# A tile for the attention sinks of 192 instead of 64 bytes: every tile behind it lies 128 bytes further on

## The chip, the cores and the metric

The kernel runs on one core of one Trainium2 chip. A core has a matrix engine (TensorE, "PE" in the profile, with its weight loads listed apart as "PEld"), a vector engine (VectorE, "DVE"), a scalar engine (ScalarE, "ACT"), GpSimd ("POOL") and SyncE ("SP", which only issues transfers here). They share an on-chip memory of 128 partitions, in which the program places its tiles by byte address within the partition, the same in all 128. The metric is the device time in microseconds of one execution; lower is better.

## The reference

The program computes two layers of a decoder trunk on 512 tokens of width 1024, in float32. Layer 0 mixes by sliding-window attention (8 query heads, 2 key heads, a learned sink per query head in the softmax's denominator) beside a short gated convolution; layer 1 by gated linear attention. Each layer then adds a gated MLP and a gated per-layer embedding:

```python
def _conv_ffn(h, w_up, conv_w, conv_b, w_down):
    u = _causal_depthwise_conv(h @ w_up, conv_w) + conv_b      # 1024 -> 2 * 2816
    gate, up = jnp.split(u, 2, axis=-1)
    return (jax.nn.gelu(gate, approximate=False) * up) @ w_down  # 2816 -> 1024
```

The sinks are eight numbers. In the softmax they are one more score per head, which has no value row.

## The kernel before

**Products in three.** A float32 operand is held as two tiles of the type float32r: a rounded high part and the rest. A product is three matmuls in a row (high by high, high by low, low by high): `mm3`, lines 162 to 168, which are lines 166, 167 and 168 of the profile. In each, the *stationary* operand (128 by 128, usually weights) is loaded into TensorE and the *moving* operand (128 partitions by 512 or 256 columns, usually activations of 512 or 256 tokens) streams past it. In the profile's groups the moving operand's tile stands first behind the arrow and the stationary one second: `ps<-four,wh` is a matmul whose moving operand lies in a tile named `four`.

**The MLP's up-projection** (`ffn`, from line 906) goes over 11 groups of 256 + 256 output columns per layer. The value half of a group is done plainly: two 128-column outputs, 8 blocks of the inner dimension each, three matmuls of 512 columns (`value`, line 950). The gate half goes through a Strassen-Winograd scheme with seven products in place of eight (`seven`, line 860): each product takes four blocks of three matmuls of 256 columns, 12 matmuls, at lines 875 to 877. Three of the seven products stream the plain normalised activations, which lie in the tiles `a0`, `a1` in layer 0 and `b0`, `b1` in layer 1; the other four stream sums and differences of them, the forms `s1` to `s4`, which `operand` (line 784) writes into tiles named `four`. TensorE's order is the order of the code (`manual_schedule` on PE); the other engines' order is a planner's.

**The down-projection** (`down`, line 1091) takes 22 activations. Those of number 0 to 7 are split into the tiles `uh` and `ul`, those of 8 to 21 into tiles `four` (`split_pair`, line 998). Numbers 0 to 13 are multiplied plainly, 512 columns a matmul. Numbers 14 to 21 go through `seven` again for four of the four column blocks in layer 0 and three of four in layer 1; there three of the seven products stream `four` tiles and four stream forms that lie in `a0`, `a1` (layer 0) or `b0`, `b1` (layer 1).

**The embedding's gate** (`ple0`, line 1284, and `ple1`, line 1326). In `ple0` the projected embedding streams from the tiles `ph0`, `pl0`, `ph1`, `pl1` of that stage's own pool. In `ple1` the weights are the moving side: half of their pieces lie in `wh`, `wl` and half in `four` tiles (`chunk`, line 1344), and `four` holds the stationary side of the projections (`proj`, line 1391).

**Where the tiles lie.** Tiles come from pools, and pools lie one behind the other in each partition. The pools `cp`, `xp`, `fp` (the `a0`, `a1`, `b0`, `b1`, `uh`, `ul` tiles), `wp` (`raw`, `wh`, `wl`), `sp` and `sm` live through the whole program; `sm` is the last of them and holds the small tiles of 32 bytes (`few`, line 79) and the sinks' tile (line 497). Behind `sm` lies the pool of whichever stage runs: `m0`, `ffn0`, `ple0`, `m1`, `ffn1`. The tiles in front of `sm` are all placed at multiples of 256 bytes, but for `mhalf`, the first, whose 128 bytes follow on 128 bytes of the program's own constants. The weights of the seven products are shifted within their tiles on purpose: `BLOCKS = (16, 48)` (line 58) puts the high part 64 bytes and the low part 192 bytes behind such a multiple (`cut_blocks`, line 812); all other weights start on one.

In `sm` there are 4 + 2 + 2 small tiles in front of the sinks', the sinks' 64 bytes, and 5 times 2 small tiles behind it: 256 + 64 + 320 = 640 bytes, which is 2.5 times 256. The pool of the running stage therefore begins at byte 157,312 = 614.5 times 256. All tiles of these pools are whole multiples of 256 bytes, so that every one of them starts 128 bytes behind a multiple of 256.

```python
def four(self, pool, dtype=F32R):                                        # line 97
    return pool.tile([P, 4, S], dtype, tag="four", name=self.nm("four"), bufs=7)

sink = self.sm.tile([P, 16], F32, name="sink", bufs=1)[:, :NQ]            # line 497
```

Of the kernel before, what the change touches and what calls it, by code (L numbers as in the profile page):

```python
# [9 lines left out]
F32 = mybir.dt.float32  # L10
# [8 lines left out]
P = 128  # L19
# [7 lines left out]
NQ, NKV, HD = 8, 2, 64  # L27
# [33 lines left out]
class Kernel:  # L61
# [367 lines left out]
    def mixer0(self):  # L429
        nc, a, tc = self.nc, self.a, self.tc  # L430
        with tc.tile_pool(name="m0", bufs=1) as mp:
# [62 lines left out]
            self.end_norm(sums=sums)  # L494
            with tc.issue_after(last[1].ins):
                C, Sn = self.rope_tables(mp)
            sink = self.sm.tile([P, 16], F32, name="sink", bufs=1)[:, :NQ]
            self.late(sink[:, :1])
            nc.gpsimd.dma_start(sink, a["hy_sinks"][0:1, :].partition_broadcast(P))
            nc.vector.tensor_scalar_mul(sink, sink, -1.0)  # L500
# [1476 lines left out]
```

## Time and profile before

| | |
|---|---|
| median of 3 runs | 1211.8 us (1211.75 to 1212.57) |
| profiled execution, its own time | 1211.79 us |
| its span, first to last instruction | 1210.0 us |
| TensorE busy | 1203.6 us (99%), 7018 matmuls |
| VectorE busy | 969.4 us (80%) |
| ScalarE busy | 667.9 us (55%) |
| GpSimd busy | 44.7 us (4%) |
| granted TensorE clock | 1.000 |

The span lacks 1.8 us of the execution's own time, which lie before the first and behind the last instruction. A matmul's duration in the profile reaches from its start to the modelled end of its pipeline, so that matmuls in a row overlap: 0.28 us stands for one of 256 columns while the next one starts 0.12 us later. How fast TensorE goes is read from the starts in the timeline, not from the durations.

### The profile page before, as it was taken

What the parts mean: (1) busy time and instruction counts of PE and PEld (TensorE: products, weight loads), DVE (VectorE), ACT (ScalarE), POOL (GpSimd) and SP (SyncE); (2) the same over time, 40 slices, a digit from 0 to 9 for tenths busy, and PEclk for the clock granted to TensorE, in tenths of its full rate; (3) what the DMA queues carried; (4) which work ended last, traced back from release to release, by engine and by line L of the source; (5) the groups of instructions that cost most, each with busy time, mean ns of one, the idle gap of its engine ahead of it and who ended that gap; (6) DMA issues with size and microseconds to landing.
All of it is one profiled execution on the core that took longest, in us unless ns stands there. A gap on an engine that the chain in (4) does not pass through costs nothing.

```text
span 1210.0 us, 17728 instructions
## 1 busy us (share of the span) xinstructions
PE 1203.6 (99%) x7018; PEld 1042.1 (86%) x7018; DVE 969.4 (80%) x1543; ACT 667.9 (55%) x1093; POOL 44.7 (4%) x64
## 2 busy tenths in 40 slices
PE   9999999999999999999999999999999999999998
PEld 8877789999999889888988988889999999888887
DVE  6786687899989986746679876778999898978595
ACT  7466565656554643534563654555665555645374
POOL 2600000000000000000100000000000000000000
PEclk9999999999999999999999999999999999999999
DMA  7232222324242332232322212322232423322501
GB/s 221 76 101 70 73 70 77 133 71 139 71 139 70 127 114 86 92 105 80 111 93 69 77 64 71 104 87 88 88 123 70 140 70 131 122 87 100 206 1 70
DMA packets 111128, 117.61 MB, mean 97 GB/s; under 512 B 2841, under 2 KB 106323, under 8 KB 111045
## 3 DMA queue, kind: packets, MB, share of 16 engines
q1 hardware_dynamic: 109680, 115.35, 28.8%
q8 instruction: 55, 0.90, 0.3%
q0 software_dynamic: 560, 0.42, 0.2%
q10 hardware_dynamic: 804, 0.70, 0.2%
q14 instruction: 29, 0.23, 0.1%
HBM read 114.37 MB, written 2.10 MB: 96 GB/s over the span
## 4 chain that ended last, share of the span: by engine, by line
PE 95%; DVE 3%; ACT 1%; issue 0%; ACTq 0%
PE ps L166 14%; PE ps L167 14%; PE ps L168 14%; PE pa L167 7%; PE pa L166 7%; PE pa L168 7%; PE ps L875 6%; PE ps L876 6%; PE ps L877 6%; PE pa L875 2%; PE pa L876 2%; PE pa L877 2%; PE ps L1374 1%; PE ps L1373 1%; PE ps L1372 1%; DVE wl L147 1%
## 5 line engine op out<-in xcount | busy, mean ns | idle before, releaser
L146 ACT ACTIVATE wh<-raw 128x1024 fp32r<-128x1024 f32 (+4 forms) x154 | 152.4, 992 | 150.4 <-PE ps L167 103.2
L147 DVE TENSOR_TENSOR wl<-raw,wh 128x1024 fp32r<-128x1024 f32 (+4 forms) x154 | 175.1, 1138 | 56.4 <-ACT wh L146 55.6
L822 ACT ACTIVATE wh<-raw 128x1024 fp32r<-128x1024 f32 x78 | 82.7, 1061 | 124.0 <-DVE raw L847 65.8
L935 DVE SCALAR_TENSOR_TENSOR zt<-z,vfa,zt 128x510 f32<-128x510 f32 (+1 forms) x176 | 130.6, 744 | 11.7 <-ACT zt L933 11.2
L823 DVE TENSOR_TENSOR wl<-raw,wh 128x1024 fp32r<-128x1024 f32 x78 | 95.3, 1222 | 20.6 <-ACT wh L822 20.5
L933 ACT ACTIVATE zt<-z,vfb 128x512 f32<-128x512 f32 x88 | 71.0, 809 | 23.9 <-DVE four L986 12.8
L166 PE MATMUL ps<-b,wh 128*128 128x512 f32 x192 | 76.6, 399 | 0.0
L167 PE MATMUL ps<-b,wh 128*128 128x512 f32 x192 | 75.1, 391 | 0.0
L168 PE MATMUL ps<-b,wl 128*128 128x512 f32 x192 | 74.9, 390 | 0.0
L167 PE MATMUL pa<-a,wh 128*128 128x512 f32 x176 | 69.1, 392 | 0.0
L167 PE MATMUL pa<-b,wh 128*128 128x512 f32 x176 | 69.0, 392 | 0.0
L166 PE MATMUL pa<-a,wh 128*128 128x512 f32 x176 | 68.8, 391 | 0.0
L166 PE MATMUL pa<-b,wh 128*128 128x512 f32 x176 | 68.8, 391 | 0.0
L168 PE MATMUL pa<-a,wl 128*128 128x512 f32 x176 | 68.7, 390 | 0.0
L168 PE MATMUL pa<-b,wl 128*128 128x512 f32 x176 | 68.6, 390 | 0.0
L876 PE MATMUL ps<-four,wh 128*128 128x256 f32 x232 | 65.3, 281 | 0.0
L875 PE MATMUL ps<-four,wh 128*128 128x256 f32 x232 | 65.1, 281 | 0.0
L877 PE MATMUL ps<-four,wl 128*128 128x256 f32 x232 | 64.8, 279 | 0.0
L166 PE MATMUL ps<-a,wh 128*128 128x512 f32 x160 | 63.6, 398 | 0.0
L167 PE MATMUL ps<-a,wh 128*128 128x512 f32 x160 | 62.4, 390 | 0.0
L168 PE MATMUL ps<-a,wl 128*128 128x512 f32 x160 | 62.4, 390 | 0.0
L166 PE MATMUL ps<-uh,wh 128*128 128x512 f32 x128 | 50.2, 392 | 0.0
(472 smaller groups left out, 3500.6 us busy)
## 6 DMA issues: line engine op xcount, KB each, us to landing
raw<-in_ffn_w_up_dram SPq DMA_DIRECT2D x44, 1024.0 KB, 5.0
raw<-in_ffn_w_down_dram SPq DMA_DIRECT2D x13, 1024.0 KB, 4.7
raw<-in_hy_w_in_dram SPq DMA_DIRECT2D x8, 1024.0 KB, 4.9
raw<-in_gla_w_in_dram SPq DMA_DIRECT2D x8, 1024.0 KB, 5.0
raw<-in_ffn_w_down_dram SPq DMA_DIRECT2D x8, 768.0 KB, 4.1
raw<-in_ple_w_gate_dram SPq DMA_DIRECT2D x6, 1024.0 KB, 4.6
raw<-in_hy_w_out_dram SPq DMA_DIRECT2D x16, 256.0 KB, 4.0
raw<-in_gla_w_out_dram SPq DMA_DIRECT2D x4, 1024.0 KB, 4.6
```

The source lines that it names most:

```text
L146: nc.scalar.activation(hv, v, AF.Copy)
L147: nc.vector.tensor_tensor(lv, v, hv.bitcast(F32), ALU.subtract)
L166: mm(out, lh, rh, start=start, stop=False, **kw)
L167: mm(out, lh, rl, start=False, stop=False, **kw)
L168: mm(out, ll, rh, start=False, stop=stop, **kw)
L822: nc.scalar.activation(h, src, AF.Copy)
L823: nc.vector.tensor_tensor(l, src, h.bitcast(F32), ALU.subtract)
L875: mm(out, wh, xh, start=first and j == 0, stop=False, **kw)
L876: mm(out, wh, xl, start=False, stop=False, **kw)
L877: mm(out, wl, xh, start=False, stop=j == ND // 2 - 1, **kw)
L933: nc.scalar.activation(y, z, AF.Identity, scale=w2[:, f : f + 1], bias=bb[:, f : f + 1])
L935: nc.vector.scalar_tensor_tensor(out=y[:, tap:], in0=z[:, : S - tap], scalar=w[:, f : f + 1], in1=y[:, tap:], op0=ALU.mult, op1=ALU.add,)
```

## The change

The sinks' tile asks for 48 numbers per partition in place of 16, of which 8 are used as before. It grows from 64 to 192 bytes.

```diff
@@ -494,7 +494,7 @@
             self.end_norm(sums=sums)
             with tc.issue_after(last[1].ins):
                 C, Sn = self.rope_tables(mp)
-            sink = self.sm.tile([P, 16], F32, name="sink", bufs=1)[:, :NQ]
+            sink = self.sm.tile([P, 48], F32, name="sink", bufs=1)[:, :NQ]
             self.late(sink[:, :1])
             nc.gpsimd.dma_start(sink, a["hy_sinks"][0:1, :].partition_broadcast(P))
             nc.vector.tensor_scalar_mul(sink, sink, -1.0)
```

No instruction is added, removed or resized. The ten small tiles behind the sinks' in `sm` and every tile of the pools `m0`, `ffn0`, `ple0`, `m1` and `ffn1` lie 128 bytes further on: the pool of the running stage begins at byte 157,440 = 615 times 256, and its tiles start at multiples of 256 bytes. The tiles in front of the sinks' stay where they are.

## The prediction

> **What bounds the kernel now.** I read the page first: busy times and the chain that ended last.
>
> ```profile
> PE 1203.6 (99%) x7018; PEld 1042.1 (86%) x7018; DVE 969.4 (80%) x1543; ACT 667.9 (55%) x1093; POOL 44.7 (4%) x64
> PE 95%; DVE 3%; ACT 1%; issue 0%; ACTq 0%
> ```
>
> TensorE is the path nearly throughout. Next the waits of TensorE alone (who waited for whom, total, times, longest), here the first two of four, and then three stretches (busy us of PE, PEld, DVE, ACT, POOL): one group of the up-projection of layer 0, and the first 20 us of its down-projection.
>
> ```profile
> PE pa L201 <- DVE mhalf L190: 1.3, 1, 1.3
> PE pa L167 <- DVE wl L1352: 0.4, 1, 0.4
> ```
>
> ```profile
> 290.45:311.26 20.81, 20.81 (x133) 18.83 (x132) 18.79 (x26) 10.71 (x16) 0.00 (x0) 1.00 0.30 102
> ...
> 415.00:425.00 10.00, 10.00 (x45) 8.13 (x45) 9.99 (x15) 4.92 (x7) 0.00 (x0) 1.00 0.46 158
> 425.00:435.00 10.00, 10.00 (x45) 8.04 (x44) 10.00 (x18) 5.84 (x8) 0.00 (x0) 1.00 0.30 105
> ```
>
> In the MLP TensorE is paced by its own matmuls. A group of the up-projection takes 20.81 us, of which VectorE works 18.79: two us of slack, no more. At the start of the down-projection VectorE is full, too.
>
> The third view is the timeline of TensorE, read by starts. Three kinds of stretches are compared: a product of 12 matmuls on `four`, the same on `a`, and 16 blocks (48 matmuls of 512 columns) on `uh` and `ul`, then on `four`.
>
> ```profile
> 301.60 0.28 PE L875 MATMUL ps<-four,wh 128*128 128x256 f32 x1
> ...
> 303.02 0.28 PE L875 MATMUL ps<-a,wh 128*128 128x256 f32 x1
> ...
> 304.39 0.40 PE L166 MATMUL pa<-a,wh 128*128 128x512 f32 x1
> ...
> 308.50 0.28 PE L875 MATMUL pa<-a,wh 128*128 128x256 f32 x1
> ...
> 309.88 0.40 PE L166 MATMUL pa<-a,wh 128*128 128x512 f32 x1
> ...
> 408.46 0.40 PE L166 MATMUL ps<-uh,wh 128*128 128x512 f32 x1
> ...
> 418.69 0.39 PE L166 MATMUL ps<-uh,wh 128*128 128x512 f32 x1
> ...
> 419.37 0.40 PE L166 MATMUL ps<-four,wh 128*128 128x512 f32 x1
> ...
> 430.56 0.40 PE L166 MATMUL ps<-four,wh 128*128 128x512 f32 x1
> ```
>
> The product on `four` takes 303.02 - 301.60 = 1.42 us, the next one on `a` 1.37, and another on `a`, behind matmuls of 512 columns as the first is, 1.38. The weights come from the same tiles at the same two offsets (64 and 192), and the shapes are equal. At 512 columns 48 matmuls take 10.91 us on `uh` and `ul` (227.3 ns each) and 11.19 on `four` (233.1 ns). So whatever streams from `four` goes about 4 ns a matmul slower at 256 columns and 6 at 512.
>
> What sets `four` apart? By the addresses its tiles start at 128 behind a multiple of 256, those of `a`, `b`, `uh`, `ul` on one. The groups by shape show whether other tiles follow that line (busy us, mean ns; a triple's other two lines have the same counts):
>
> ```profile
> L876 PE MATMUL ps<-four,wh 128*128 128x256 f32 x232 | 65.3, 281 | 0.0
> L876 PE MATMUL ps<-a,wh 128*128 128x256 f32 x120 | 33.3, 278 | 0.0
> L876 PE MATMUL pa<-four,wh 128*128 128x256 f32 x116 | 32.6, 281 | 0.0
> L167 PE MATMUL ps<-ul,wh 128*128 128x512 f32 x128 | 50.1, 391 | 0.0
> L167 PE MATMUL ps<-four,wh 128*128 128x512 f32 x112 | 44.2, 395 | 0.0
> L876 PE MATMUL ps<-four,t 128*128 128x256 f32 x88 | 24.8, 282 | 0.0
> ...
> L167 PE MATMUL ps<-wl,a 128*128 128x512 f32 x32 | 12.5, 390 | 0.0
> ...
> L168 PE MATMUL pa<-wh,four 128*128 128x512 f32 x16 | 6.3, 395 | 0.0
> ...
> L167 PE MATMUL ps<-pl,wh 128*128 128x512 f32 x16 | 6.3, 394 | 0.0
> ...
> L1373 PE MATMUL ps<-four,a 128*128 128x512 f32 x14 | 5.5, 394 | 0.0
> ...
> L1373 PE MATMUL ps<-four,b 128*128 128x512 f32 x12 | 4.7, 395 | 0.0
> ...
> L1373 PE MATMUL ps<-wl,a 128*128 128x512 f32 x12 | 4.7, 390 | 0.0
> ```
>
> Every group with an operand in a shifted pool shows 394 to 395 ns at 512 columns, also `pl`, of another pool and stage, and also `pa<-wh,four`, where `four` is the stationary side. Groups wholly in front of the small pool show 390 to 391. Two points bear on the cause. The tiles `wl` start at 0, 256 and 512 behind a multiple of 2048, and stream at 390: 256 is alignment enough, and `four` will have that. And the last two blocks before 419.37 stream a `ul` that lies in a tile `R` of the pool `sp`, at 152,576, only 4,736 bytes in front of the first `four`: 419.37 - 418.69 = 0.68 us a block, the quick pace. A border by height in the memory would have to fall by chance between those two.
>
> **The change part by part.** Nothing is issued anew, removed or queued differently, and no wait is added; only addresses move.
>
> *The 256-column products on `four`.* 232 + 116 + 88 = 436 per line, three lines: 1308 matmuls, 109 products of 12. Each goes from 1.42 us to 1.37 or 1.38: 0.04 to 0.05 saved, 4.4 to 5.5 us in all; I take 4.9. In the up-projection that is four products a group, 0.18 us, so a group falls to about 20.63 us, still 1.8 above VectorE's 18.79. It counts in full there.
>
> *The 512-column matmuls with a shifted moving tile in the down-projection and in `ple0`.* 3 x 112 + 3 x 16 = 384. By the rows' means 395 against 391 less what rounding hides, say 3 ns, by the timeline 5.8: 1.2 to 2.2 us; I take the middle, 1.7.
>
> *`ple1`.* 3 x (14 + 12) moving and 3 x 16 stationary, 126 matmuls, 4 to 6 ns each: 0.5 to 0.7 us where TensorE paces the stage. The wait of 0.4 us above lies there, so part may be lost: 0 to 0.7, taken 0.3.
>
> *VectorE and ScalarE on shifted tiles.* Nothing:
>
> ```profile
> L857 DVE TENSOR_TENSOR raw<-raw 128x512 f32<-128x512 f32 x26 | 17.8, 685 | 0.1
> ...
> L932 DVE TENSOR_TENSOR z<-z,R 128x512 f32<-128x512 f32 x22 | 15.0, 682 | 0.0
> ```
>
> `raw` is aligned, `z` shifted, and the two times agree within 3 ns. The slack of 2 us a group would cover it; without that cover 3 ns on some 20 operations is 0.06 us a group.
>
> *Plain float32 matmuls of the mixers* (attention's scores, the linear attention's levels, transposes). The nearest rows compare a transpose of an aligned tile with one of a shifted tile:
>
> ```profile
> L1380 PE MATMUL pa<-cf,xT 128*128 128x128 f32 x32 | 4.1, 272 | 0.0
> L1827 PE MATMUL pa<-cf,sc 128*128 128x128 f32 x32 | 4.1, 272 | 0.0
> ```
>
> No difference, so I take 0. The bound: these groups hold some 500 records; at 5.8 ns either way that is 2.9 us.
>
> *Transfers into shifted tiles.* At the start x lands in `xin`, which moves, among pieces of the weights for `raw`, which doesn't (same size, median us to landing):
>
> ```profile
> xin<-in_x_dram SPq DMA_DIRECT2D x8, 256.0 KB, 4.8
> ...
> raw<-in_hy_w_in_dram SPq DMA_DIRECT2D x4, 256.0 KB, 5.7
> ```
>
> The shifted ones land no later than the aligned ones. I take 0, and 0.9 us either way as the bound.
>
> The sum: 4.9 + 1.7 + 0.3 = 6.9 us. The profiled execution's own time is 1211.79 (its span 1210.0 and 1.8 around it), the median of the runs 1211.8, so the sum needs no correction: **1204.9 us**.
>
> One rule speaks against all this. The Trainium skill, "SBUF — State Buffer", section "Specifications (TRN2)", gives the memory lines of 16 bytes, and its section "Who interferes with whom" gives TensorE two independent read ports and says that it waits on nobody. By that a start at 128 is as good as one at 0, and the sum would be 0 and the time 1211.8. The rows above (1.42 against 1.37 us) don't fit it, since both kinds of product read whole lines of 16 bytes.
>
> **The rivals.**
>
> *The gain is made and given back* (VectorE takes over). For it: the two full rows of the down-projection, 9.99 and 10.00 of 10 us. There VectorE makes the forms that the products at 443 us need, and TensorE arriving 0.3 us sooner may wait for them; ScalarE's copies between products may eat as much again in each of the seven column blocks that run by `seven`. Against it: no wait of TensorE on VectorE in that stretch in the list. I price it as all of the 512-column gain and a fifth of the other: 4.9 x 0.8 + 0.3 = 4.2, so 1207.6 us.
>
> *Nothing happens.* The change wouldn't do what it says if `four` were slow for where it is and not for its phase: for its height in the memory. For it: all shifted tiles are also the highest ones, and no tile of the profile is high and aligned. Against it: the `ul` at 152,576. The time is 1211.8 us. The skill's lines of 16 bytes would end here, too.
>
> *Equal phases collide: slower.* Moving and stationary operands that both start on a multiple of 256 are read together in the keys' and values' projection, where `wh` streams past `a`. Twelve matmuls of 256 columns in a row, from the timeline:
>
> ```profile
> 17.10 0.28 PE L168 MATMUL pa<-wh,a 128*128 128x256 f32 x1
> ...
> 18.54 0.28 PE L168 MATMUL pa<-wh,a 128*128 128x256 f32 x1
> ```
>
> 1.44 us for 12, worse than the 1.42 on the shifted `four`. If the products on `four` came to that pace and the 512-column ones gained nothing, the price would be 109 x 0.02 = 2.2 us: 1214.0. It decides once a product takes longer than 1.42. Against it: the weights of the products stand at 64 and 192, so that phases never become equal there, and with 512 columns `uh` and `wh` have equal phases and run at 227.3 ns.
>
> **How the numbers follow.** The forecast gets 0.80, the gain given back 0.10, nothing 0.07, slower 0.03. A measurement of this kernel tells about 0.2% (2.4 us) from no change. The forecast and the first rival lie beyond that: faster 0.90. Nothing, and most of the collision at +2.2 us, lie within: I put 0.08 there and 0.02 on slower. The range goes down to 1202.8, where the two main terms come at their upper ends (5.5 and 2.2), `ple1` at 0.7, and 0.6 of the unseen bounds helps, and up to 1208.5, where the gain is given back and the start costs its bound of 0.9 more.
>
> **What would show it.** In the changed kernel's timeline a product on `four` should take 1.37 to 1.38 us and 48 matmuls of 512 columns on `four` about 10.9 us; a group of the up-projection about 20.63 us; the groups `ps<-four`, `ps<-pl` and `pa<-wh,four` should read 390 to 392 ns at 512 columns. VectorE's and ScalarE's means should stay as they are. If the products stay at 1.42 us, the phase isn't the cause, and the forecast falls. If they quicken and the time doesn't, TensorE must show new waits, first in the down-projections.

## The result and the profile after

The changed kernel takes **1205.3 us** (median of 6 runs, 1204.9 to 1205.7) beside 1211.8 us before (6 runs): a ratio of 0.9946, 95% interval 0.9935 to 0.9957. The profiled execution took 1205.4 us with a span of 1203.6, against 1211.79 and 1210.0 before. Every engine has the same instructions in the same order.

The page of the changed kernel, busy times and the chain that ended last; below it TensorE's waits (total, times, longest), in full:

```profile
PE 1196.3 (99%) x7018; PEld 1036.0 (86%) x7018; DVE 968.4 (80%) x1543; ACT 665.5 (55%) x1093; POOL 44.7 (4%) x64
...
PE 82%; DVE 12%; DMA 2%; ACT 2%; issue 1%; ACTq 0%; DVEq 0%
```

```profile
PE pa L201 <- DVE mhalf L190: 1.3, 1, 1.3
PE ps L875 <- ACT ps L896: 0.7, 3, 0.3
PE pa L167 <- DVE wl L1352: 0.6, 1, 0.6
PE ps L166 <- DVE kT L1564: 0.2, 1, 0.2
PE pa L167 <- DVE wl L147: 0.2, 1, 0.2
```

TensorE is 7.3 us less busy. TensorE's share of the chain falls from 95% to 82% and VectorE's rises from 3% to 12%. The second wait is new: a product waits for a copy that ScalarE makes from one accumulator to another (L896). In ScalarE's queue that copy stands behind the gelu (L1064), which had waited for VectorE, as here for the wait at 317 us:

```profile
316.01 1.06 ACT L1064 ACTIVATE zt<-zt 128x1024 f32<-128x1024 f32 x1 [1.08 <-DVE zt L935]
316.98 0.37 ACT L896 COPY ps<-ps 128x256 f32<-128x256 f32 x1
```

So something was given back.

The timeline of TensorE after, by starts: a product on `four` behind matmuls of 512 columns, block by block, the product on `a` behind it, and 16 blocks of 512 columns on `four` in the down-projection.

```profile
279.43 0.28 PE L875 MATMUL ps<-four,wh 128*128 128x256 f32 x1
279.79 0.28 PE L875 MATMUL ps<-four,wh 128*128 128x256 f32 x1
280.13 0.28 PE L875 MATMUL ps<-four,wh 128*128 128x256 f32 x1
...
280.81 0.28 PE L875 MATMUL ps<-a,wh 128*128 128x256 f32 x1
...
282.18 0.40 PE L166 MATMUL pa<-a,wh 128*128 128x512 f32 x1
...
417.70 0.39 PE L166 MATMUL ps<-four,wh 128*128 128x512 f32 x1
...
428.58 0.39 PE L166 MATMUL ps<-four,wh 128*128 128x512 f32 x1
```

The product on `four` takes 280.81 - 279.43 = 1.38 us (1.42 before), the one on `a` 1.37, as before. The 48 matmuls of 512 columns take 10.88 us (11.19 before), 226.7 ns each. The groups by shape agree:

```profile
L876 PE MATMUL ps<-four,wh 128*128 128x256 f32 x232 | 64.2, 277 | 0.0
...
L167 PE MATMUL ps<-four,wh 128*128 128x512 f32 x112 | 43.6, 390 | 0.0
...
L168 PE MATMUL pa<-wh,four 128*128 128x512 f32 x16 | 6.3, 391 | 0.0
...
L167 PE MATMUL ps<-pl,wh 128*128 128x512 f32 x16 | 6.2, 389 | 0.0
```

Now five groups of the up-projection of layer 0, the third to the seventh, cut at the starts of their first products (length and busy us of PE, PEld, DVE, ACT, POOL). First before (the third and the fifth), then after (all five):

```profile
228.01:248.82 20.81, 20.81 (x133) 18.83 (x132) 20.22 (x29) 12.33 (x19) 0.00 (x0) 1.00 0.31 102
...
269.64:290.45 20.81, 20.81 (x133) 18.83 (x132) 20.75 (x30) 13.69 (x21) 0.00 (x0) 1.00 0.31 102
```

```profile
227.29:247.87 20.58, 20.58 (x133) 18.63 (x132) 19.99 (x28) 12.35 (x18) 0.00 (x0) 1.00 0.31 103
247.87:268.46 20.59, 20.59 (x133) 18.62 (x132) 20.00 (x29) 11.83 (x17) 0.00 (x0) 1.00 0.31 103
268.46:289.05 20.59, 20.59 (x134) 18.63 (x132) 20.53 (x30) 13.26 (x20) 0.00 (x0) 1.00 0.32 103
289.05:309.87 20.82, 20.82 (x134) 18.54 (x132) 18.75 (x25) 10.51 (x14) 0.00 (x0) 1.00 0.31 102
309.87:331.23 21.36, 21.10 (x133) 18.62 (x132) 19.27 (x26) 11.27 (x17) 0.00 (x0) 1.00 0.30 100
```

Most groups now take 20.59 us, 0.22 less than before. But VectorE has no room in the fifth: 20.53 of 20.59 us. The two groups behind it take 20.82 and 21.36 us; the first of them shows no idle time of TensorE, because modelled durations overlap, so the list of waits (0.7 us) tells less than the lengths do. Layer 1 shows the same shape (20.72 and 21.17 us), and there the last group with the plain down-projection takes 48.48 us, where layer 0's takes 47.74.

Two questions follow. Is the quicker pace due to where the moving operand starts, as the prediction has it? And does VectorE open the new waits?

### The profile page after: what moved, and what is told of

Its sections match the earlier page's. It is cut to its first block, busy times and chain, and to the rows that moved or that the text cites. A ratio compares the mean times of both kernels' runs of the same rounds, so it can differ in the third digit from the quotient of the medians.

```text
span 1203.6 us, 17728 instructions
## 1 busy us (share of the span) xinstructions
PE 1196.3 (99%) x7018; PEld 1036.0 (86%) x7018; DVE 968.4 (80%) x1543; ACT 665.5 (55%) x1093; POOL 44.7 (4%) x64
## 4 chain that ended last, share of the span: by engine, by line
PE 82%; DVE 12%; DMA 2%; ACT 2%; issue 1%; ACTq 0%; DVEq 0%
PE ps L166 14%; PE ps L167 14%; PE ps L168 14%; PE pa L167 5%; PE pa L166 5%; PE pa L168 5%; PE ps L875 4%; PE ps L877 4%; PE ps L876 4%; DVE zt L935 3%; DMA raw<-in_ffn_w_up_dram 2%; DVE wl L823 2%; PE pa L875 2%; PE pa L877 2%; PE pa L876 2%; DVE wl L147 1%
## 5 line engine op out<-in xcount | busy, mean ns | idle before, releaser
L935 DVE SCALAR_TENSOR_TENSOR zt<-z,vfa,zt 128x510 f32<-128x510 f32 (+1 forms) x176 | 130.7, 744 | 11.7 <-ACT zt L933 11.2
```

What stands on the lines that cost most here:

```text
L935: nc.vector.scalar_tensor_tensor(out=y[:, tap:], in0=z[:, : S - tap], scalar=w[:, f : f + 1], in1=y[:, tap:], op0=ALU.mult, op1=ALU.add,)
```

## The experiments

Times are medians. The kernel before ran beside each and gave 1211.5 to 1211.8 us. "Phase" is a start in the memory modulo 256.

**Other phases of the moved tiles.** The kernel before, with a sinks' tile of 32, of 64 and of 80 numbers. The stage's pools then start at phase 192, at 64, and at 128 again but 256 bytes higher than before.

```diff
-            sink = self.sm.tile([P, 16], F32, name="sink", bufs=1)[:, :NQ]
+            sink = self.sm.tile([P, 32], F32, name="sink", bufs=1)[:, :NQ]   # 64; 80
```

> The sinks' tile has 128 bytes: the stage pools begin 192 behind a multiple of 256 (kernel before: 128, changed kernel: 0). Theory A (a moving operand that starts anywhere inside a stretch of 256 bytes needs one stretch more): as slow as before, 1211 to 1212.5 us, a product of 12 on `four` 1.42 us. Theory C (the cost shrinks with the distance to the next multiple, or the unit is 64 bytes): 1205 to 1209 us, a product at 1.37 to 1.40.

> The sinks' tile has 256 bytes: the stage pools begin 64 behind a multiple of 256. Theory A: 1211 to 1212.5 us, a product on `four` 1.42 us. Theory C: between 1205 and 1211 us. A result unlike that at 192 would mean that the phase against the weights' 64 and 192 matters, not the start alone.

> The sinks' tile has 320 bytes: everything behind it lies 256 bytes further on than in the kernel before, at the same phase of 128. Theory A: as before, 1211.8 us (1211.3 to 1212.3), a product on `four` 1.42 us. If the unit were 512 bytes or more, or if any shift away from the old place helped: under 1209 us.

Measured: 1211.97 us at 192 (ratio 1.0003, 0.9993 to 1.0012), 1213.19 at 64 (1.0012, 1.0003 to 1.0021), 1211.46 at 128 higher up (0.9998, 0.9988 to 1.0007). A product on `four`, the product on `a` behind it and the next matmul, first at 192, then at 64:

```profile
300.91 0.28 PE L875 MATMUL ps<-four,wh 128*128 128x256 f32 x1
...
302.32 0.28 PE L875 MATMUL ps<-a,wh 128*128 128x256 f32 x1
...
303.72 0.40 PE L166 MATMUL pa<-a,wh 128*128 128x512 f32 x1
```

```profile
302.25 0.28 PE L875 MATMUL ps<-four,wh 128*128 128x256 f32 x1
...
303.68 0.28 PE L875 MATMUL ps<-a,wh 128*128 128x256 f32 x1
...
305.10 0.39 PE L166 MATMUL pa<-a,wh 128*128 128x512 f32 x1
```

On `four` 1.41 and 1.43 us: neither phase brings the gain. The rival of height fell with the result, since the quick tiles lie higher than the slow ones did; the third run adds that a move by itself changes nothing. But the products on `a` are slower too, 1.40 and 1.42, and `a` was not moved. At 256 columns a matmul's own moving start can't be the whole cause.

At 512 columns the picture is another. The groups by shape, first at 192, then at 64:

```profile
L167 PE MATMUL ps<-four,wh 128*128 128x512 f32 x112 | 44.2, 394 | 0.0
...
L168 PE MATMUL pa<-wh,four 128*128 128x512 f32 x16 | 6.3, 393 | 0.0
```

```profile
L167 PE MATMUL ps<-four,wh 128*128 128x512 f32 x112 | 43.6, 390 | 0.0
...
L168 PE MATMUL pa<-wh,four 128*128 128x512 f32 x16 | 6.3, 395 | 0.0
```

By the starts of the first 72 matmuls on `four` in layer 0's down-projection, one takes 233.2 ns with `four` at 128, 233.3 at 192, 229.2 at 64 and 226.7 at 0. So a start at 64 brings more than half of the gain at 512 columns, and the loss on the products of 256 columns outweighs it. The weights of these matmuls start on multiples of 256 in every run here. In `pa<-wh,four` it is the other way round: the moving `wh` starts on such a multiple and `four` is the stationary side. That group reads 391 ns with `four` at 0, 395 at 64 and 128, and 393 at 192. As distances (the stationary start less the moving one, modulo 256) the two agree: 0 is quick, 192 lies between, 64 and 128 are slow. The differences are of a few ns, and no run was made to test this.

**Which tiles bring the gain.** An unused tile of 128 bytes at the head of the MLP's pools alone: in the kernel before it moves those pools (`ple1` works in the second one) and nothing else, in the changed kernel it moves them back.

```diff
-            self.mlp = fp
+            self.mlp = fp; fp.tile([P, 32], F32, name=f"pad{i}")
```

> Sinks' tile as before; an unused tile of 128 bytes stands first in the two MLP pools, so that only the tiles of `ffn0` and `ffn1` start on multiples of 256, while those of `m0`, `ple0` and `m1` stay at 128. Theory A: nearly the whole gain, less 0.3 us for `ple0` and what the start of the program moved: 1205.4 to 1206.2 us. If the mixers or the transfers of x carried part of the gain: above 1207 us.

> The mirror image: the changed kernel with an unused tile of 128 bytes first in the two MLP pools, so that `m0`, `ple0` and `m1` start on multiples of 256 and only the MLP's tiles at 128. Theory A: 1211.0 to 1211.8 us (gain 0.3 of `ple0` at most and a few tenths at the start). If mixers or transfers carried part: under 1210.5 us.

Measured: the MLP alone 1205.52 us (0.9949, 0.9935 to 0.9964), all but the MLP 1211.67 us (1.0001, 0.9991 to 1.0010). The gain is that of the MLP's pools. In the second kernel the groups by shape show the two pools apart:

```profile
L167 PE MATMUL ps<-four,wh 128*128 128x512 f32 x112 | 44.2, 395 | 0.0
...
L167 PE MATMUL ps<-pl,wh 128*128 128x512 f32 x16 | 6.2, 389 | 0.0
```

`ple0` has the quick pace and the MLP has not; `ple0`'s 48 matmuls at some 5 ns are 0.2 us, too little to show in the time.

**The weights' two places exchanged**, in the kernel before.

```diff
-BLOCKS = (16, 48)
+BLOCKS = (48, 16)
```

> The kernel before (`four` at 128) with the high and low parts of the product's weights exchanged in their offsets: high at 192, low at 64. Measured from the moving operand, each part then lies as in the changed kernel (64 and 192 further on). Theory A (the moving operand's own start): 1211.3 to 1212.3 us, products on `four` at 1.42. Theory R (the distance between the two operands): 1205 to 1207 us, products on `four` at 1.37 to 1.38.

Measured: 1208.79 us (0.9977, 0.9968 to 0.9986).

```profile
300.90 0.28 PE L875 MATMUL ps<-four,wh 128*128 128x256 f32 x1
...
302.28 0.28 PE L875 MATMUL ps<-a,wh 128*128 128x256 f32 x1
...
303.70 0.40 PE L166 MATMUL pa<-a,wh 128*128 128x512 f32 x1
```

With `four` still at 128, its product takes 1.38 us; `a`, at 0, takes 1.42. So an operand at 128 can go at the quick pace and one at 0 at the slow. For the products of 256 columns the cause that the prediction gave falls here. (The 72 matmuls of 512 columns keep their 233.2 ns; their weights don't use these places.) I put another in its place: what counts is the distance between the stationary and the moving start, modulo 256.

**Equal phases**, in the changed kernel: the weights' places at 0, as the moving operands are.

```diff
-BLOCKS = (16, 48)
+BLOCKS = (0, 0)
```

> The changed kernel with the offsets of the products' weights at 0 and 0 in place of 64 and 192, so that moving and stationary operands both start on multiples of 256. Theory E (equal phases collide with 256 columns, as in the keys' and values' projection at 1.44 us for 12): all 203 products go from 1.37 to 1.44 us, 1215 to 1220 us. If only the moving operand's start counts: 1205 to 1206 us.

Measured: 1215.73 us (1.0033, 1.0021 to 1.0046).

```profile
302.44 0.28 PE L875 MATMUL ps<-four,wh 128*128 128x256 f32 x1
...
303.88 0.28 PE L875 MATMUL ps<-a,wh 128*128 128x256 f32 x1
...
305.32 0.40 PE L166 MATMUL pa<-a,wh 128*128 128x512 f32 x1
```

1.44 us for both, the pace that the prediction read off the keys' and values' projection. With both operands at 0 the 256-column products are at their slowest: the prediction's third rival exists, in this kernel and not in the changed one.

**The exchange in the changed kernel**, to test the distance against the own start: the same edit as in the exchange above, made in the changed kernel.

> The changed kernel with the two places of the 256-column weights exchanged (BLOCKS = (48, 16), so the high part lies 192 and the low part 64 bytes into a line of 256, with the activations at 0). Theory of the distance (stationary start less moving start, modulo 256): every 256-column product is now at (192, 64) instead of (64, 192), those on `four` as they were in the kernel before and those on `a` and `b` as they were with the exchange made in the kernel before. So the products on `four` take 1.42 us again and most of those on `a` and `b` 1.42 instead of 1.37 us; the 512-column matmuls do not use these places and keep 680 ns for three. Gain of 512 columns kept, gain of 256 columns lost, and some 2.4 to 3 us more on `a` and `b`: 1211.5 to 1213.5 us, a group of the up-projection at about 20.9 to 21.0 us. Theory of the prediction (the start of the moving operand alone): nothing that it counts has changed, 1205 to 1206 us, 20.6 us a group.

Measured: 1204.52 us (0.9940, 0.9926 to 0.9953).

```profile
279.65 0.28 PE L875 MATMUL ps<-four,wh 128*128 128x256 f32 x1
...
281.02 0.28 PE L875 MATMUL ps<-a,wh 128*128 128x256 f32 x1
...
282.38 0.40 PE L166 MATMUL pa<-a,wh 128*128 128x512 f32 x1
```

1.37 and 1.36 us: as quick as any. For the products of 256 columns my second theory falls as well, by 7 us and more; the matmuls of 512 columns, whose weights the exchange doesn't touch, still fit it. The products of the timelines above, side by side:

| kernel | `four` at | `a` at | weights, high/low | on `four`, us | on `a` behind it, us |
|---|---|---|---|---|---|
| before | 128 | 0 | 64/192 | 1.42 | 1.37 |
| after | 0 | 0 | 64/192 | 1.38 | 1.37 |
| sinks 32 | 192 | 0 | 64/192 | 1.41 | 1.40 |
| sinks 64 | 64 | 0 | 64/192 | 1.43 | 1.42 |
| exchanged, before | 128 | 0 | 192/64 | 1.38 | 1.42 |
| exchanged, after | 0 | 0 | 192/64 | 1.37 | 1.36 |
| equal phases, after | 0 | 0 | 0/0 | 1.44 | 1.44 |

The fifth and sixth rows hold the point. The product on `a` reads the same phases in both (0, and 192/64), its instructions are the same, and it takes 1.42 us in one and 1.36 in the other. What differs is the product ahead of it. The tiles of the other engines moved as well, but the kernel of the fifth row shows the same within itself: by their starts, the 22 products on `a` and `b` of its up-projection that stand behind matmuls of 512 columns on the same tiles take 1.36 or 1.37 us, and the 44 behind a product on `four` 1.42 or 1.43, but for one of 1.54. (They write other accumulators, which makes no such difference in the kernel of the sixth row.) So the pace of a product isn't settled by its own addresses; it depends on the starts that both operands have *and on what TensorE came from*. The single blocks point the same way: after the change, the first block of the product on `four` takes 279.79 - 279.43 = 0.36 us and the second 0.34; it begins slowly and then runs quick. In the kernel before, the same product doesn't come to the quick pace within its four blocks (from 301.60 to 303.02, which the prediction shows, the steps are 0.35, 0.35, 0.36 and 0.36 us):

```profile
301.95 0.28 PE L875 MATMUL ps<-four,wh 128*128 128x256 f32 x1
302.30 0.28 PE L875 MATMUL ps<-four,wh 128*128 128x256 f32 x1
302.66 0.28 PE L875 MATMUL ps<-four,wh 128*128 128x256 f32 x1
```

What these runs share is that the kernels in which the moving operands of all products start at 0 and the weights at 64 and 192, in either order, are quick throughout; no other common phase was run. What holds the slow pace, and by what rule a change of phase leads into it, stays open. The product ahead isn't all of it either: in the run at 192 the seven products on `a` and `b` with weights in `t` take 1.36 us behind a product on `four`, the 44 with weights in `wh` 1.40.

**VectorE's products given to GpSimd**, to take load off VectorE in the changed kernel. Gate times value of groups 5 to 11 (L986) moves to the other engine.

```diff
-                nc.vector.tensor_tensor(x, g, y, ALU.mult)
+                nc.gpsimd.tensor_tensor(x, g, y, ALU.mult)
```

> The changed kernel with the products of gate and value of the groups 4 to 10 (line 986, seven of 1.22 us per layer) on GpSimd in place of VectorE. If the new waits of TensorE in the up-projection (some 1.8 us over both layers) come from VectorE's fullness, they go: 1203.3 to 1204.5 us. If they come from the loads or from ScalarE's order, or if GpSimd holds VectorE up: 1205.3 us or more.

Measured: 1213.7 us (1.0013, 1.0004 to 1.0023), 8.4 us more than the changed kernel. First the operation on VectorE in the changed kernel, by groups; then its durations on GpSimd (min, median, max in ns):

```profile
L986 DVE TENSOR_TENSOR four<-zt,zt 128x1024 f32<-128x1024 f32 x12 | 14.7, 1225 | 0.6
```

```profile
L986 POOL TENSOR_TENSOR four<-zt,zt x12: 2387/2392/2406, 297.4 to 1026.1; 128x1024 f32<-128x1024 f32 x12
L986 POOL TENSOR_TENSOR zt<-zt,zt x2: 10926/10932/10937, 419.9 to 1045.1; 128x1024 f32<-128x1024 f32 x2
```

The product takes 2.39 us there in place of 1.23, and 10.9 us for the two last ones. It sits in a chain (gelu, product, the next activation into the same tile), and TensorE waits longer (2.3 us in all for ScalarE's copy at L900, for which the changed kernel has no wait). The run says nothing on VectorE's load, because it made the chain longer as it made the load smaller.

**A third of the convolution left out**, in the kernel before and in the changed one. Here the last of the three taps behind the up-projection isn't computed, so that VectorE has one operation (L935) less for every tile that is convolved.

```diff
-                for tap, w in ((1, w1), (2, w0)):
+                for tap, w in ((1, w1),):
```

> The kernel before with one of the three taps of the MLP's convolution left out (the value two tokens back is not added), which takes 88 operations of 0.74 us off VectorE. Nothing in the up-projection waited for VectorE before: 1211.0 to 1212 us, a group at 20.81 us.

> The changed kernel with the same tap left out. If VectorE's fullness takes back some 1.8 us of the gain, every group of the up-projection comes to 20.59 us and the distance to the kernel before with the same tap left out is 7.8 to 8.5 us: about 1203.5 us. If the waits have another cause: a distance of 6.4 us, about 1205.2 us.

Measured: 1211.47 us before the change (0.9999, 0.9990 to 1.0009) and 1203.14 after it (0.9932, 0.9917 to 0.9946). The fifth and the seventh group after:

```profile
268.55:289.14 20.59, 20.59 (x134) 18.62 (x133) 18.56 (x26) 13.27 (x21) 0.00 (x0) 1.00 0.31 103
309.72:330.31 20.59, 20.59 (x134) 18.62 (x132) 15.98 (x21) 10.98 (x17) 0.00 (x0) 1.00 0.31 103
```

With room on VectorE (18.56 us in the fifth group) no group is longer than 20.59 us, and the wait on L896 is gone. VectorE costs the kernel before nothing that shows; it costs the changed kernel 1205.32 - 1203.14 = 2.2 us, or 1.9 by the two differences (6.46 with all taps, 8.33 without).

**VectorE's gathered work spread out**, in the changed kernel, nothing left out. The planner has put all eight subtractions that split activations 0 to 7 (L106, 0.68 us each) into groups 3 to 5, the full ones. Here all but two stand behind the product of a later group, one a group.

```diff
-                nc.vector.tensor_tensor(x, g, y, ALU.mult)
+                self.last = nc.vector.tensor_tensor(x, g, y, ALU.mult)
...
-                for f in (6, 7):
-                    split_one(f)
+                for f in (7,):
+                    with tc.issue_after(self.last.ins): split_one(f)
...
-                    if 4 <= d < groups - 1:
-                        split_one(d - 4)
+                    if 2 <= d < groups - 2:
+                        with tc.issue_after(self.last.ins) if d > 3 else ExitStack(): split_one(d - 2)
```

> The changed kernel with VectorE's eight subtractions that split the first eight activations (L106 ul<-u,uh, 0.68 us each) no longer gathered in groups 3 to 5 of the up-projection (234 to 282 us in layer 0, where VectorE is busy 20.0 to 20.5 of 20.6 us) but two in group 3 and one behind the product of each group from the fifth on, so that no group has more than about 19.4 us of VectorE. If those gathered subtractions make VectorE late and so open the waits of TensorE behind them (the groups of 20.82, 21.37, 20.72 and 21.17 us): all groups at 20.59 to 20.65 us, no wait on the copy of L896, and 1203.3 to 1204.5 us in all; that beats the changed kernel by 0.07 to 0.16%. If the waits come from the order of ScalarE's queue alone (its copy behind the gelu), they stay, and the time is 1205.3 us. If a subtraction behind each product delays what follows it in every group: above 1205.6 us.

Measured: 1203.79 us (1202.9 to 1206.5 in 5 runs; ratio 0.9938, 0.9925 to 0.9950). The fifth, sixth and seventh group, and the chain:

```profile
268.94:289.52 20.58, 20.58 (x133) 18.62 (x132) 18.68 (x26) 11.30 (x16) 0.00 (x0) 1.00 0.32 103
289.52:310.12 20.60, 20.60 (x133) 18.63 (x132) 19.49 (x27) 11.95 (x19) 0.00 (x0) 1.00 0.31 103
310.12:330.71 20.59, 20.59 (x133) 18.62 (x132) 19.69 (x27) 11.72 (x19) 0.00 (x0) 1.00 0.32 104
```

```profile
PE 94%; DVE 4%; ACT 1%; issue 0%; POOL 0%; ACTq 0%; DVEq 0%
```

All groups take 20.58 to 20.60 us, the wait on L896 is gone, TensorE has 94% of the chain again, and the long 48.48 us of layer 1 are 47.74. The same work in another place makes the waits vanish. The edit moves ScalarE's copies that belong to the subtractions, too; but the run without the tap changed VectorE's work alone. By both runs together the fullness of VectorE in groups 3 to 5 is what opened the waits. Of the kernels here that compute everything this one has the lowest median: it is 1.5 us below the changed kernel's, though the two intervals overlap, so the profile shows the gain better than the times do. The exchange of the weights' places with this spread was not run.

## Why the prediction was right, and where it was not

The time, 1204.9 against 1205.3, was right. That it was so near was in part luck: the sum has two errors of opposite sign, and its cause doesn't hold for the products of 256 columns, the largest term.

- **The products on `four`**: 1.37 to 1.38 us expected, 1.38 measured behind 512 columns. The means of the groups by shape fell from 281 to 277 ns. Those directly behind another product came to 1.36. Summed over all starts the 109 products fell from 155.2 to 150.0 us in the kernel with the work spread, where the waits on VectorE are gone: 5.2, where 4.9 was taken. The 94 products on `a` and `b`, for which nothing was counted, gained as well: from 130.1 to 129.3 us there, and the mean of the group on `a` in the changed kernel from 278 to 276 ns.
- **The 512-column matmuls** were a term sized too small. 1.2 to 2.2 us was the range and 1.7 was taken; 48 of them fell from 11.19 to 10.88 us, 6.5 ns each, and 384 x 6.5 ns = 2.5 us; summed over all starts the 384 gained 2.3. The mean of two readings should have been the timeline's alone, since the groups' means are durations that overlap.
- **`ple1`**: 0.3 expected, 0 to 0.7 allowed. From its first matmul to the first of its last stretch of 256 columns it takes 52.10 us (1144.25 to 1196.35) in place of 52.61 (1150.13 to 1202.74), 0.5 less. VectorE's operations kept their means (L857 685 ns, L932 683), the transposes their 272 ns, as expected.
- **"So a group falls to about 20.63 us, still 1.8 above VectorE's 18.79. It counts in full there"** is the step that failed in the sum. The group shown was the sixth. In the third to the fifth VectorE already worked 20.22 to 20.75 of 20.81 us before the change. A group came down further than expected, to 20.59, and then the next ones ran into VectorE. Without the waits the gain is 8.0 us (work spread) or 8.3 (tap left out); they took 1.6 to 1.9 of it back. The forecast of 6.9 stands between that and the 6.5 measured.
- **The first rival**, a gain given back to VectorE, happened in part: some 1.9 us where it had 2.7, in the up-projection and not at the start of the down-projection where it was placed.
- **"256 is alignment enough, and `four` will have that"**, with the moving start as the cause, is the step that failed in the reasons, for the products of 256 columns. The runs with exchanged weights show that a start at 128 can be quick there and a start at 0 slow. The forecast held because the change put all moving operands of the products at 0, where the rows for `a` had shown the quick pace with these weights; why that pace holds is open. At 512 columns the start of `four` does set the pace (226.7 ns at 0, 229.2 at 64, 233.2 and 233.3 at 128 and 192), but as `pa<-wh,four` slows down with the stationary side moved, the moving start alone isn't the cause there, either; the distance of the two starts fits.
- **Height** is excluded by the result: the tiles lie higher and are quicker. **Equal phases** collide as the prediction priced them (1.44 us), but only if the weights are put there.
- By the Trainium skill, "SBUF — State Buffer", section "Who interferes with whom", TensorE's two read ports are independent and it waits on nobody. The runs don't bear out what the prediction drew from it, that the places make no difference: exchanging the two places of the weights alone, in the kernel before, changed a product on `a` from 1.37 to 1.42 us.

## What to carry to other kernels

Before counting a saving on the bounding engine in full, take the windows of *every* repetition of a stage, and look for the one where the next engine is full: an average group, or one picked by chance, hides it. Where matmuls run back to back by the thousand, it is worth trying to keep all moving operands on one phase of 256 bytes and the stationary ones on others (here 0 against 64 and 192 was the quick choice at 256 columns), and to time the products in their order: a placement that is quick behind one product can be slow behind another. And a planner's hoisted side work is worth a look once the main engine gets quicker; moving it later cost nothing and brought back what had been lost.

## What was not expected of the hardware

The pace of a product of 256-column matmuls depends on what ran before it. The same product of 12 matmuls, at the same places in memory, took 1.42 us behind a product on a tile at phase 128 and 1.36 us behind one at phase 0. Over a whole product the quickest and the slowest placement lie 6% apart (1.36 and 1.44 us). At 512 columns equal phases were the quickest placement (226.7 ns a matmul with both at 0), at 256 columns the slowest. And GpSimd took 10.9 us for a product of two tiles of 128 by 1024, written over one of its inputs, where products into a third tile took it 2.39 us a few groups earlier; why is open.
